# Seven block products instead of eight for the sparse values and six gate tiles, in a hybrid attention block on one core

## The chip, the core and the metric

The kernel runs on one core of a Trainium2 chip. Its engines are TensorE (PE in the profile, its weight loads PEld), VectorE (DVE), ScalarE (ACT), GpSimd (POOL) and SyncE (SP), which issues most DMAs. The metric is the device time of one execution in microseconds (us), lower is better.

## The reference, cut to what matters

One layer on x of 512 tokens by 1024 channels, float32. A normalised input h feeds one combined projection; dense attention (branch a) and sparse top-128 attention (branch b), 8 heads each, give outputs that are gated, projected and summed.

```
h = rmsnorm(x, norm_g)
(q_lat, c_kv, k_rope, z_a, q_b, k_b, v_b, z_b, q_idx, k_idx, w_idx, gate_a, gate_b) = split(h @ w_in)
y_a = mla_attention(...) * silu(z_a)
# sparse heads: score by an indexer, keep 128 keys, add a position bias
logits = q_b . k_sel * scale + bias ;  p = softmax(logits) ;  y_b = (p @ v_sel) * silu(z_b)
merged = sigmoid(gate_a) * (y_a @ w_o_a) + sigmoid(gate_b) * (y_b @ w_o_b)
out = rmsnorm(x + merged @ w_out)
```

## The kernel before

Everything lies transposed in SBUF (channels on partitions, 512 tokens along the free dimension). Each float32 operand is split in two rounded parts, hi (a ScalarE copy, line 291) and lo (a subtraction on VectorE, line 317, or on GpSimd, line 319). A product takes three matmuls per 128-row block of the contraction, hi.hi, hi.lo and lo.hi (`mm3`, line 394; the matmul itself is line 389). The normalised input is eight such pairs, `hT[0..7]`, tiles `s_h`.

The order of all instructions is made by a planner when the program is built (`Flow.run`, line 178): generator functions yield steps, each with one or more engines that could do it and a cost; the step that could start first is emitted. On the chip every engine then works through its list in that fixed order and waits on semaphores. A step with several engines goes to the one with the earliest planned end; `BOTH` is VectorE or GpSimd.

TensorE's filler is a queue of weight tiles (`QUEUE`, line 1641). `fetcher` (line 833) loads each into one of 4 raw buffers of 512 KB (`raw`), `splitter` (line 843) makes the hi and lo parts (`s_w`), `multiplier` (line 853) runs the products. One tile of a projection (`proj`, line 861) is 128 output channels: 24 matmuls of 512 columns with weights `s_w` and moving data `s_h`. The queue holds eight gate tiles of branch a (`ga`) and eight of branch b (`gb`), each stored as tanh in `s_sig`; eight silu tiles (`za`, `zb`); key and query tiles of the sparse heads (`sb`); and the sparse values (`vb`, `values`, line 918) in two halves of 96 matmuls of 256 columns, here with `s_h` as weights and `s_w` moving. Between the filler run, at higher priority, the heads: logits, softmax, four transposes by a matmul with the identity (line 406), the product with the values. Before the sparse heads VectorE does the top-128 search (lines 786 and 787, 16 rounds for each of three row tiles).

A sparse head (`dsa_head`, line 1236) adds a bias tile to the logits and takes their maximum in one VectorE operation (line 1248), negates the maximum (line 336), exponentiates on ScalarE with the row sum, takes the reciprocal (line 1142) and scales the row by it (`normalise`, on VectorE line 347 or GpSimd line 350). Its bias tile plus mask is prepared by `dsa_base` (line 1223). Its query and key operands come from `dsa_jobs` (line 1195): for each head of a pair separately the 64 rows are split by ScalarE and VectorE (qhi and s_op), the keys then copied to the other 64 partitions by DMA.

After the last projection (`hT_done`, line 881, key "projections") come the branch output products `branch_out` (line 1335), for a and then b, eight tiles of 12 matmuls each, and the output product, already done with seven block products (`output`, line 1491). `y_gate` (line 1275) splits the gated head outputs for them.

Of the kernel before, what the change touches and what calls it, by code (L numbers as in the profile page):

```python
# [79 lines left out]
class Step:  # L80


    moves = 0.0
    pair = False
    pbias = None
# [45 lines left out]
class Flow:  # L131
# [46 lines left out]
    def run(self, stop=None):  # L178
        while self.threads:
            if stop and stop():  # L180
                return
            moved = False
            for t in sorted(self.threads, key=lambda t: t.prio):
                if isinstance(t.req, Get):
                    b = t.req.pool.give(t.req)
                    if b is not None:
                        self.advance(t, b)
                        moved = True
                elif isinstance(t.req, Until) and t.req.cond():
                    self.advance(t, None)  # L190
                    moved = True
            if moved:
                continue
            best = None
            for t in self.threads:
                if isinstance(t.req, Step):
                    for i, (eng, dur, emit) in enumerate(t.req.options):
                        s = self.start(t.req, eng)
                        key = (s + BIAS * t.prio, t.prio)
                        if len(t.req.options) > 1:  # L200
                            fin = s + dur + {"POOL": self.pbias if t.req.pbias is None else t.req.pbias, "ACT": ABIAS}.get(eng, 0.0)
# [12 lines left out]
            if eng == "SP":  # L214

                self.free["SP"] = s + 0.05
                self.hw = max(self.hw, s) + (0.65 if step.ins and step.outs else 0.475)
                self.dma = max(self.dma, self.hw + 0.65) + dur
                end = self.dma + (2.2 if step.ins and step.outs else 1.0)
# [12 lines left out]
            self.advance(t, None)  # L232
# [1 line left out]

RAW_LAG = {"DVE": 0.125, "POOL": 0.1, "ACT": 0.1}
BIAS = 0.01
ABIAS = 0.0
TC_ARGS = {}


# [1 line left out]
def tile_block(ctx: ExitStack, tc: tile.TileContext, a: dict, out: bass.AP, bias_dram: bass.AP):  # L242
# [11 lines left out]
    rounded = {"w", "wo", "xg", "h", "qs", "th", "lat", "op", "qpe", "ph", "last", "vv", "ys", "mg", "oh"}  # L254
    uid = [0]

    def fresh(b, cls):
# [202 lines left out]
    rb = fixed("rb", [64, NH])  # L460
    rbs = fixed("rbs", [64, NH], F32R)
    TOK = [slice(t * P, (t + 1) * P) for t in range(NT)]
    SWAP = [(k + 16) % 32 for k in range(32)]
    done = set()

# [357 lines left out]


    jobs = []

    class Job:
        def __init__(self, src, widths, body, cls="w", cap=None, prep=None):
# [14 lines left out]
    def splitter():  # L843
        for job in jobs:
            yield Until(lambda: job.raw is not None)
            if job.prep:
                spawn(job.prep(job), 9)
# [13 lines left out]
    def proj(name, c, take, prio):  # L861
# [14 lines left out]
        left[0] += 1  # L876
        Job(a[name][c], [512, 512], body)

    left = [0]

    def hT_done():
# [5 lines left out]

    sig = {}

    def gate(name, c):  # L890


        def take(ps):
            s = yield slot("sig")
            yield act(s.all.f, ps.all, AF.Tanh, scale=0.5)
            put(ps)
            sig[name, c] = s

        proj(name, c, take, 12)

    zt = {}

    def silu2(name, c):


        def take(ps):
# [3 lines left out]
            put(ps)  # L910
            zt[name, c] = z

        proj(name, c, take, 11)


    vv, vv_users = {}, {}
# [221 lines left out]
        put(ps, t)  # L1138
        done.add((br, h))

    def normalise(p, mx):
        yield Step([("DVE", 0.07, lambda: nc.vector.reciprocal(mx.tile[:, 3:4], mx.tile[:, 2:3]))], [mx], [mx])  # L1142
        yield scale_by(p, p, mx[:, 3:4], NORM)

    def prob_tiles(cls, cap):
        s = []
# [45 lines left out]
    lanes = {"a": set(), "b": set()}  # L1192


    def dsa_jobs(j):
        def take_q(ps):
            yield Until(lambda: ("a", NH - 1, 0) in operands)
            for b in range(2):
                own, oth = slice(64 * b, 64 * b + 64), slice(64 - 64 * b, 128 - 64 * b)
                q = yield Get(QHI)  # L1200
                yield act(q[own, :], ps[own, :], AF.Copy, scale=HD ** -0.5)
                yield stt(q[oth, :], ps[own, :], HD ** -0.5, q[own, :].f, ALU.mult, ALU.subtract)
                operands["b", 2 * j + b, 0] = q
            put(ps)

        def take_k(ps):
            for b in range(2):
                own, oth = slice(64 * b, 64 * b + 64), slice(64 - 64 * b, 128 - 64 * b)
                kh = yield slot("op")
                kl = yield slot("op")  # L1210
                yield act(kh[own, :], ps[own, :])
                yield lo_part(kl[own, :], ps[own, :], kh[own, :])
                yield dma(kh[oth, :].f, kh[own, :].f)
                yield dma(kl[oth, :].f, kl[own, :].f)
                operands["b", 2 * j + b, 1] = (kh, kl)
            put(ps)

        proj("w_kb", j, take_k, 8)
        proj("w_qb", j, take_q, 8)

    bases = {}

    def dsa_base(h):
# [4 lines left out]
        yield dma(bias.all.f, bass.AP(bias_dram.tensor, h * NREL + 1, [[1, P], [1, S]]))  # L1228
        slots, probs = yield from prob_tiles("p", 6)
        for i in range(NT):  # L1230
            n = P * (i + 1)
# [4 lines left out]
    def dsa_head(h):  # L1236
# [7 lines left out]
        def soft(i, ps):  # L1244
            n = P * (i + 1)
            mx = yield Get(SMALL)
            p = probs[i]
            step = Step([("DVE", 0.1 + 0.00104 * n, lambda: nc.vector.tensor_tensor_reduce(
                p.ap, ps.tile[:, :n], p.ap, op0=ALU.add, op1=ALU.max, scale=1.0, scalar=FILL,
                accum_out=mx.tile[:, 0:1]))], [mx, p.buf], [ps])  # L1250
# [24 lines left out]
    def y_gate(br, j):  # L1275
# [21 lines left out]


    left1, left2, left3, left4, base = {}, {}, {}, {}, {}
    LO, HI = slice(0, 256), slice(256, 512)  # L1300

    def split_m(x, n, dst, key):
        hi = yield slot("mg")
# [267 lines left out]

    outs = [(p, c) for p, n in ((1, 2), (7, 4), (2, 2), (6, 2), (5, 4), (4, 2), (3, 2)) for c in range(n)]
    for item in QUEUE.split():
        kind, n = item[:2], item[2:]
        if kind == "ga" or kind == "gb":
            gate("w_" + kind, int(n))
        elif kind == "za" or kind == "zb":
            silu2("w_" + kind, int(n))
        elif kind == "pe":
            qpe_job()  # L1580
        elif kind == "ma":
            mla_job(int(n))
        elif kind in ("va", "vb"):
            values(kind[1], int(n))
        elif kind == "sb":
            dsa_jobs(int(n))
        elif kind == "ou":
            out_job(*outs.pop(0))
    for m in range(2 * NK):
# [27 lines left out]
    for br in "ab":  # L1617
        for j in range(4):
            spawn(y_gate(br, j), 8)
    spawn(final_loads(), 20)  # L1620
    spawn(output(), 15)
    run()


LATE = 0.5
PSQ = 0.0
PSET = 0.0
NORM = ('DVE', 'POOL')
NWARM = 7
XAT = 1  # L1630
QPOOL = 0
PHCAP = 4
WCAP = 8
TCAP = 5
# [89 lines left out]
```

## Time and profile before

| | us |
|---|---|
| median of 3 runs | 439.57 (439.42 to 441.98) |
| the profiled execution | 439.49 |
| its span, first to last instruction | 437.7 |
| PE, DVE, ACT, POOL busy | 426.2, 345.1, 244.6, 125.3 |

The granted TensorE clock is 0.998 of full speed. Times in the profile count from the span's start. In a group's row "x768 | 189.4, 394" means 768 instructions, 189.4 us in which at least one of them ran, and 394 ns for one from its start to its end; matmuls overlap, so what one costs in a stream is the distance between starts.

### The profile page before, as it was taken

How to read it: one execution, taken by the hardware profiler on the slowest of the kernel's cores; microseconds unless marked ns; L12 is line 12 of the kernel's file. 1: busy time of each engine (PE TensorE's matmuls, PEld its weight loads, DVE VectorE, ACT ScalarE, POOL GpSimd, SP SyncE). 2: the span in 40 equal slices, each digit the busy share in tenths (PEclk: the TensorE clock that was granted, in tenths of full speed). 3: DMA queues.
4: the chain of work that ended last, by engine and by line, in shares of the span. 5: the costliest groups of instructions: out<-in, count | busy, mean ns of one | idle time of the engine just before them, and what ended most of it. 6: DMA issues, size and time to landing. Idle time of an engine off the chain costs nothing.

```text
span 437.7 us, 6862 instructions
## 1 busy us (share of the span) xinstructions
PE 426.2 (97%) x2219; PEld 364.7 (83%) x2219; DVE 345.1 (79%) x810; ACT 244.6 (56%) x546; POOL 125.3 (29%) x150
## 2 busy tenths in 40 slices
PE   8999999999999999999999999999999999999994
PEld 5899878888887888878899888998888888888883
DVE  5599589999999999794343977835776686999995
ACT  6976877557472757364333654734565553345633
POOL 2256966544555634000003120050000011001452
PEclk9999999999999999999999999999999999999999
DMA  8973441725337361414541216234116445538405
GB/s 260 393 251 92 111 146 55 204 82 138 98 84 209 79 185 33 120 43 144 145 148 45 73 73 144 82 112 133 60 50 216 168 152 185 179 111 288 145 1 192
DMA packets 26500, 59.45 MB, mean 136 GB/s; under 512 B 4072, under 2 KB 4600, under 8 KB 26464
## 3 DMA queue, kind: packets, MB, share of 16 engines
q1 hardware_dynamic: 25744, 58.05, 43.2%
q0 software_dynamic: 576, 0.83, 0.7%
q8 instruction: 17, 0.28, 0.3%
q14 instruction: 19, 0.16, 0.1%
q10 hardware_dynamic: 144, 0.13, 0.1%
HBM read 48.39 MB, written 2.12 MB: 115 GB/s over the span
## 4 chain that ended last, share of the span: by engine, by line
PE 73%; DVE 13%; DMA 4%; ACT 4%; issue 2%; POOL 1%; SPq 1%; POOLq 0%; DVEq 0%; ACTq 0%
PE ps L389 67%; PE ps L406 4%; DVE mask L787 3%; DVE sm L786 3%; DMA s_op<-s_op 2%; DVE sm L1163 1%; DMA raw<-w_kvl 1%; DMA s_op<-kpel 1%; ACT junk L300 1%; PE ps L764 1%; SPq L416 1%; DVE s_ph L317 1%; PE ps L1182 1%; DVE qhi L328 1%; DVE s_op L328 1%
## 5 line engine op out<-in xcount | busy, mean ns | idle before, releaser
L389 PE MATMUL ps<-s_h,s_w 128*128 128x512 f32 x768 | 189.4, 394 | 0.0
L389 PEld LDWEIGHTS ps<-s_h,s_w 128*128 128x128 f32 x768 | 140.9, 188 | 26.7 <-issue 0.2
L319 POOL TENSOR_TENSOR s_w<-raw,s_w 128x512 fp32r<-128x512 f32 (+2 forms) x38 | 45.1, 1197 | 99.0 <-DMA raw<-w_out 64.3
L291 ACT CAST s_w<-raw 128x512 fp32r<-128x512 f32 (+3 forms) x114 | 64.3, 591 | 4.2 <-PE ps L389 2.1
L317 DVE TENSOR_TENSOR s_w<-raw,s_w 128x512 fp32r<-128x512 f32 (+2 forms) x76 | 49.2, 670 | 12.2 <-ACT s_w L291 11.8
L319 POOL TENSOR_TENSOR s_p<-s_bias,mask 128x128 f32<-128x128 f32 (+3 forms) x19 | 14.4, 785 | 102.9 <-DMA s_bias<-bias_scratch 90.3
L389 PE MATMUL ps<-s_ys,s_w 128*128 128x512 f32 x192 | 43.7, 389 | 0.0
L389 PEld LDWEIGHTS ps<-s_ys,s_w 128*128 128x128 f32 x192 | 36.0, 188 | 7.5
L389 PE MATMUL ps<-s_wo,s_mg 128*128 128x512 f32 (+1 forms) x156 | 33.0, 373 | 0.0
L389 PE MATMUL ps<-s_w,s_xg 128*128 128x328 f32 (+1 forms) x192 | 32.4, 324 | 0.0
L389 PEld LDWEIGHTS ps<-s_w,s_xg 128*128 128x128 f32 x192 | 31.5, 188 | 0.8 <-DVE s_w L317 0.2
L389 PEld LDWEIGHTS ps<-s_wo,s_mg 128*128 128x128 f32 x156 | 27.6, 188 | 5.2
L787 DVE MATCH_REPLACE8 mask<-sm,mask 128x256 f32<-128x256 f32 (+2 forms) x48 | 25.9, 541 | 0.0
L786 DVE MAX8 sm<-mask 128x8 f32<-128x256 f32 (+2 forms) x48 | 25.6, 549 | 0.3
L300 ACT ACTIVATE s_p<-ps,sm 128x128 f32<-128x128 f32 (+3 forms) x32 | 16.8, 527 | 15.2 <-DVE sm L1163 13.4
L389 PE MATMUL ps<-s_w,s_h 128*128 128x256 f32 x192 | 23.8, 284 | 0.0
L389 PEld LDWEIGHTS ps<-s_w,s_h 128*128 128x128 f32 x192 | 23.4, 192 | 0.2
L300 ACT ACTIVATE s_p<-s_p,sm 128x128 f32<-128x128 f32 (+3 forms) x32 | 17.8, 558 | 9.9 <-DVE sm L336 9.8
L406 PE MATMUL ps<-ident,s_p 128*128 128x128 f32 x160 | 22.9, 273 | 0.0
L300 ACT ACTIVATE s_sig<-ps 128x512 f32<-128x512 f32 x16 | 9.6, 597 | 22.7 <-PE ps L389 22.5
L350 POOL TENSOR_SCALAR s_p<-s_p,sm 128x128 f32<-128x128 f32 (+3 forms) x31 | 16.1, 527 | 19.0 <-DVE sm L1142 18.8
L389 PE MATMUL ps<-s_lat,s_w 128*128 128x512 f32 x78 | 21.4, 398 | 0.0
(164 smaller groups left out, 723.5 us busy)
## 6 DMA issues: line engine op xcount, KB each, us to landing
raw<-w_out SPq DMA_DIRECT2D x18, 512.0 KB, 4.2
raw<-w_ga SPq DMA_DIRECT2D x8, 512.0 KB, 4.3
raw<-w_gb SPq DMA_DIRECT2D x8, 512.0 KB, 3.6
raw<-w_o SPq DMA_DIRECT2D x16, 256.0 KB, 3.8
s_op<-s_op SPq DMA_DIRECT2D x28, 128.0 KB, 2.3
s_x<-xT SPq DMA_DIRECT2D x8, 256.0 KB, 5.4
s_xn<-x SPq DMA_DIRECT2D x8, 256.0 KB, 5.4
raw<-w_za SPq DMA_DIRECT2D x4, 512.0 KB, 4.2
```

The lines of the kernel that those rows point to most:

```text
L291: nc.scalar.copy(dst.ap, src.ap)
L300: nc.scalar.activation(dst.ap, src.ap, func, **kw)
L317: opts.append(("DVE", 0.07 + 0.00104 * x.n, lambda: nc.vector.tensor_tensor(dst.ap, x.ap, y.ap, op=op)))
L319: opts.append(("POOL", 0.15 + 0.0021 * x.n, lambda: nc.gpsimd.tensor_tensor(dst.ap, x.ap, y.ap, op=op)))
L328: lambda: nc.vector.scalar_tensor_tensor(dst.ap, x.ap, sc(s), y.ap, op0=op0, op1=op1))],
L350: lambda: nc.gpsimd.tensor_scalar(dst.ap, x.ap, s.ap, 1.0, ALU.mult, ALU.mult)))
L389: nc.tensor.matmul(ps.ap, l.ap, r.ap, start=start and i == 0, stop=stop and i == len(pairs) - 1, skip_group_check=more)
L406: nc.tensor.transpose(d.ap, s.ap, ident.tile)
L416: return Step([("SP", n / 360000.0, lambda: nc.sync.dma_start(d, s))], bufs(dst), bufs(src))
L764: yield pe(0.005 + n / 2400, [ps.all], [qs[h].all, ks[0].all], lambda: nc.tensor.matmul(ps.tile[:, :n], qs[h].tile[:96, TOK[i]], ks[0].til ...
L786: yield Step([("DVE", t, lambda: nc.vector.max(m8.tile, work.tile))], [m8], [work])
L787: yield Step([("DVE", t, lambda: nc.vector.match_replace(work.tile, m8.tile, work.tile, MARK))], [work], [m8])
```

## The change

- **Values.** The two halves `vb0`, `vb1` become one job `VB` (`values2`): the 512 x 1024 by 1024 x 512 product is cut in 2 by 2 blocks and done with seven block products (numbers 1 to 7) instead of eight, each 24 matmuls of 256 columns.
- **Six gate tiles.** `gb0` to `gb5` become three pairs (`proj2`); the two weight tiles of a pair are the blocks of one side, seven products of 12 matmuls of 256 columns instead of 48 of 512. `gb6`, `gb7` stay as they were.
- **What seven products need.** `input_sums` makes eight sums and differences of halves of `hT` (tiles `s_tmp`) and their hi and lo parts (`s_hs`); `prep` sums the raw weights in place and in `s_wsum`, and splits seven blocks where there were four; `seven` combines the products (`s_pair`), some in PSUM by accumulating into a bank that another engine has just read, some by VectorE additions.
- **Sparse heads.** Line 1248 gives negated logits and their minimum, so the negation of the maximum goes; the scaling by the reciprocal may go to VectorE or ScalarE, no more to GpSimd (`NORM_B`). Queries and keys of a pair are split by one operation of 128 partitions each instead of two of 64, and more DMAs move the halves in place.
- **Gates of branch a.** All eight (`AWAY`) are written to DRAM after their tanh and read back after the last projection (`fetch_gates`).
- One of three copies of each index query goes by GpSimd's queue (`QPOOL`), the planner counts 1.5 us more for the bias load, `y_gate` waits for the last pair instead of the last projection, and the queue has another order.

How the counts of instructions change, from the two built programs (TensorE: operands moving, weights; the rest of TensorE's list is the same in number):

```
PE   ps<-s_h,s_w   128x512: 768 -> 624      DVE  s_wsum, raw sums 512: 8 -> 27 (one more on POOL)
PE   ps<-s_h,s_w   128x256:   0 -> 108      DVE  s_tmp sums 512: 0 -> 6, 256: 0 -> 13 ; s_hs 512: 0 -> 7
PE   ps<-s_hs,s_w  128x256:   0 -> 144      DVE  s_pair<-ps 256: 0 -> 15, 512: 0 -> 5
PE   ps<-s_w,s_h   128x256: 192 ->  72      DVE  s_w<-raw or s_wsum 512: 62 -> 73
PE   ps<-s_w,s_hs  128x256:   0 ->  96      DVE  s_p<-s_bias,mask: 13 -> 29 (POOL 19 -> 3)
ACT  s_p<-s_p,sm (scaling): 0 -> 18         DVE  s_p<-s_p,sm (scaling): 33 -> 14
ACT  s_w, s_hs casts 512: 90 -> 113         DVE  sm<-sm (negation): 32 -> 0
SP   s_op<-s_op: 28 -> 36, qhi: 0 -> 12     DVE  qhi, s_op splits of 64 partitions: 16 -> 0, of 128: 0 -> 8
SP   bias_scratch<-s_sig: 0 -> 8, back: 0 -> 8 ; s_qs<-s_th: 24 -> 16 (POOL 0 -> 8)
```

```diff
+    def input_sums():
+        yield Until(lambda: sums_due[0] in done)
+        for k in range(4):
+            f = []
+            for i in (k, k + 4):
+                t = yield slot("tmp", TCAP)
+                yield soon(tt(t.all.f, hT[i][0].all.f, hT[i][1].all.f, ALU.add, BOTH))
+                f.append(t)
+            x, y = (t.all.f for t in f)
+            yield soon(tt(x[:, HI], x[:, LO], x[:, HI], ALU.subtract, BOTH))
...
+    def proj2(first, second):
...
+        def prep(job):
...
+            yield from split_t(1, b11)
+            t = yield slot("wsum")
+            t3 = t.all.f
+            yield soon(tt(t3, b22, b12, ALU.subtract, BOTH))
+            yield soon(tt(b12, b12, b11, ALU.subtract, BOTH))
+            yield soon(tt(b11, t3, b11, ALU.add, BOTH))
+            yield from split_t(6, b11)
+            yield from split_t(2, b21)
+            yield from split_t(7, t3)
...
+    def seven(times, part, c11, c21, c12, c22, end):
...
+        x = yield bank("mm")
+        yield from times(1, x)
+        spawn(take("1", act(c22, part(x))), 0)
+        y = yield bank("mm")
+        yield from times(6, y)
+        yield Until(lambda: "1" in sums)
+        spawn(take("u2", add(c12, y, c22)), 0)
+        yield from times(2, x, True)
+        spawn(take("c11", act(c11, part(x)), x), 0)
+        yield Until(lambda: "u2" in sums)
+        yield from times(7, y, True)
+        spawn(take("u3", add(c21, y, c22), y), 0)
+        z = yield bank("mm")
+        yield from times(5, z)
+        yield Until(lambda: "u3" in sums)
+        spawn(take("c22", add(c22, z, c21)), 0)
+        v = yield bank("mm")
+        yield from times(4, v)
+        yield Until(lambda: "c22" in sums)
+        spawn(take("c21", add(c21, v, c21), v), 0)
+        yield from times(3, z, True)
+        spawn(take("c12", add(c12, z, c12), z), 0)
...
+    def fetch_gates():
+        yield is_done("projections")
+        for c in away:
+            yield is_done(("spilt", c))
             s = yield slot("sig")
+            yield dma(s.all.f, spilt(c))
+            sig["w_ga", c] = s
...
-            yield ts(mx[:, 1:2], mx[:, 0:1], -1.0, None, ALU.mult)
-            yield act(p, p, AF.Exp, bias=mx[:, 1:2], scale=1.0, accum=mx[:, 2:3])
-            yield from normalise(p, mx)
+            yield act(p, p, AF.Exp, bias=mx[:, 1:2], scale=-1.0, accum=mx[:, 2:3])
+            yield from normalise(p, mx, NORM_B)
...
-        yield is_done("projections")
+        yield is_done("pairs")
...
-QUEUE = 'ga0 ga1 pe ma0 va0 ga2 za0 ma1 va1 ga3 za1 ma2 ga4 za2 ma3 ga5 za3 sb0 zb0 ga6 ga7 sb1 zb1 vb0 gb1 gb0 sb2 zb2 vb1 gb2 sb3 gb3 zb3 gb4 gb5 ou gb6 ou gb7 ou'
+QUEUE = 'ga0 ga1 pe ma0 va0 ga2 za0 ma1 va1 ga3 za1 ma2 ga4 za2 ma3 ga5 za3 sb0 zb0 ga6 ga7 sb1 VB GB0 GB1 sb2 zb1 GB2 GB3 sb3 zb2 GB4 GB5 ou zb3 gb6 ou gb7 ou'
```

More of the change, by code (lines that the diff above doesn't have):

```diff
@@ L80 @@
 class Step:
+    abias = 0.0
+    late = 0.0
     moves = 0.0
@@ L218, in run @@
                 self.dma = max(self.dma, self.hw + 0.65) + dur
-                end = self.dma + (2.2 if step.ins and step.outs else 1.0)
+                end = self.dma + (2.2 if step.ins and step.outs else 1.0) + step.late
             else:
@@ L253, in tile_block @@
     slots = ctx.enter_context(tc.tile_pool(name="slots", bufs=1, reuse_waits="tile"))
[L254 removed]
+    rounded = {"w", "wo", "xg", "h", "qs", "th", "lat", "op", "qpe", "ph", "last", "vv", "ys", "mg", "oh", "hs"}
     uid = [0]
@@ L846, in splitter @@
             if job.prep:
-                spawn(job.prep(job), 9)
+                if job.body:
+                    yield from job.prep(job)
+                else:
+                    spawn(job.prep(job), 9)
                 continue
@@ L877, in proj @@
         Job(a[name][c], [512, 512], body)
+    hs = {}
+    def input_sums():
[8 more added lines that the diff above has]
+            yield soon(tt(x[:, HI], x[:, LO], x[:, HI], ALU.subtract, BOTH))
+            yield soon(tt(y[:, HI], y[:, HI], x[:, HI], ALU.subtract, BOTH))
+            yield soon(tt(x[:, LO], y[:, HI], x[:, LO], ALU.add, BOTH))
+            yield soon(tt(y[:, LO], y[:, LO], y[:, HI], ALU.subtract, BOTH))
+            for i in range(2):
+                hi = yield slot("hs")
+                lo = yield slot("hs")
+                yield act(hi.all, f[i].all.f)
+                yield soon(lo_part(lo.all, f[i].all.f, hi.all))
+                put(f[i])
+                hs[k, i] = (hi, lo)
@@ new lines, in side, with hold, split_t, times @@
+    def side(n, k):
+        if n in (1, 2, 4):
+            return cut(hT[k if n == 1 else k + 4], HI if n == 4 else LO)
+        return cut(hs[k, n in (3, 6)], HI if n in (6, 7) else LO)
+    def proj2(first, second):
+        parts, raws = {}, []
+        def hold(job):
+            raws.append(job.raw)
+            yield Until(lambda: True)
+        def split_t(n, x):
+            hi = yield slot("w", PCAP)
+            lo = yield slot("w", PCAP)
+            yield act(hi.all, x)
+            yield soon(lo_part(lo.all, x, hi.all))
+            parts[n] = (hi, lo)
+        def prep(job):
+            yield Until(lambda: raws)
+            raws.append(job.raw)
+            b11, b21 = raws[0][:, :S], raws[0][:, S:]
+            b12, b22 = raws[1][:, :S], raws[1][:, S:]
+            yield from split_t(1, b11)
[7 more added lines that the diff above has]
+            yield from split_t(7, t3)
+            put(t)
+            yield from split_t(5, b12)
+            yield soon(tt(b21, b21, b11, ALU.subtract, BOTH))
+            yield from split_t(4, b21)
+            put(raws[0])
+            yield from split_t(3, b22)
+            put(raws[1])
+        def times(n, ps, more=False):
+            for k in range(4):
+                yield Until(lambda: n in parts and (k, 0) in hs and (k, 1) in hs)
+                yield mm3(ps[:, :256], cut(parts[n], slice(k * P, k * P + P)), side(n, k), k == 0 and not more, k == 3, more)
+            put(*parts[n])
+        def body(job):
+            out = []
+            for _ in range(2):
+                out.append((yield slot("pair")))
+            views = [o.all.f[:, c] for o in out for c in (LO, HI)]
+            yield from seven(times, lambda ps: ps[:, :256], views[0], views[1], views[2], views[3], lambda: spawn(give(out), 3))
+            pair_done()
+        def give(out):
+            for o, (name, c, take, prio) in zip(out, (first, second)):
+                spawn(take(o), prio)
+            return
+            yield
+        left[0] += 1
+        pairs_left[0] += 1
+        Job(a[first[0]][first[1]], [512, 512], None, prep=hold)
+        Job(a[second[0]][second[1]], [512, 512], body, prep=prep)
@@ new lines, in seven, with take, add @@
+    def seven(times, part, c11, c21, c12, c22, end):
+        sums = set()
+        def take(key, step, release=None):
+            yield step
+            if release:
+                put(release)
+            sums.add(key)
+            if len(sums) == 7:
+                end()
+        def add(dst, ps, y):
+            return tt(dst, part(ps), y, ALU.add)
+        x = yield bank("mm")
[20 more added lines that the diff above has]
+        spawn(take("c12", add(c12, z, c12), z), 0)
@@ L879, in tile_block, with in_pairs @@
+    pairs_left = [0]
+    waiting = []
+    def in_pairs(item):
+        waiting.append(item)
+        if len(waiting) == 2:
+            proj2(*waiting)
+            waiting.clear()
     left = [0]
@@ L911, in take @@
             zt[name, c] = z
-        proj(name, c, take, 11)
+        how(name, c, take, 11)
     vv, vv_users = {}, {}
@@ L1192, in tile_block, with dsa_jobs @@
     lanes = {"a": set(), "b": set()}
-    def dsa_jobs(j):
+    def dsa_jobs(j, how=proj):
         def take_q(ps):
             yield Until(lambda: ("a", NH - 1, 0) in operands)
[L1198 to L1203, printed above, removed]
-            put(ps)
-        def take_k(ps):
[L1207 to L1215, printed above, removed]
-            put(ps)
-        proj("w_kb", j, take_k, 8)
-        proj("w_qb", j, take_q, 8)
+            q = yield Get(QHI)
+            q2 = yield Get(QHI)
+            lo = yield slot("op")
+            yield from split_scaled(q.all, lo.all, ps.all, HD ** -0.5)
+            put(ps)
+            first, second = slice(0, 64), slice(64, 128)
+            yield dma(q2[second, :].f, q[second, :].f)
+            yield dma(q2[first, :].f, lo[second, :].f)
+            yield dma(q[second, :].f, lo[first, :].f)
+            put(lo)
+            operands["b", 2 * j, 0] = q
+            operands["b", 2 * j + 1, 0] = q2
+        def take_k(ps):
+            first, second = slice(0, 64), slice(64, 128)
+            pairs = []
+            hi = yield slot("op")
+            lo = yield slot("op")
+            yield act(hi.all, ps.all)
+            yield lo_part(lo.all, ps.all, hi.all)
+            put(ps)
+            for part in (hi, lo):
+                k = yield slot("op")
+                for rows in (first, second):
+                    yield dma(k[rows, :].f, part[first, :].f)
+                yield dma(part[first, :].f, part[second, :].f)
+                pairs.append(k)
+            operands["b", 2 * j, 1] = tuple(pairs)
+            operands["b", 2 * j + 1, 1] = (hi, lo)
+        how("w_kb", j, take_k, 8)
+        how("w_qb", j, take_q, 8)
@@ L1227, in dsa_base @@
         bias = yield slot("bias")
-        yield dma(bias.all.f, bass.AP(bias_dram.tensor, h * NREL + 1, [[1, P], [1, S]]))
+        step = dma(bias.all.f, bass.AP(bias_dram.tensor, h * NREL + 1, [[1, P], [1, S]]))
+        step.late = 1.5
+        yield step
         slots, probs = yield from prob_tiles("p", 6)
@@ L1628 @@
 NORM = ('DVE', 'POOL')
+NORM_B = ('DVE', 'ACT')
+NORM_BIAS = -0.5
 NWARM = 7
 XAT = 1
-QPOOL = 0
+QPOOL = 1
 PHCAP = 4
```

141 lines of the change are left out of this document (123 added, 18 removed).

## The prediction

> **What bounds the kernel now.** I read the page first: span, busy time by engine, the chain that ended last.
>
> ```profile
> span 437.7 us, 6862 instructions
> PE 426.2 (97%) x2219; PEld 364.7 (83%) x2219; DVE 345.1 (79%) x810; ACT 244.6 (56%) x546; POOL 125.3 (29%) x150
> PE 73%; DVE 13%; DMA 4%; ACT 4%; issue 2%; POOL 1%; SPq 1%; POOLq 0%; DVEq 0%; ACTq 0%
> ```
>
> TensorE bounds it. The question is where it idles and where the other engines have room for new work, so next the windows: length, then PE, PEld, DVE, ACT, POOL busy with instruction counts.
>
> ```profile
> 0.00:20.00 20.00, 17.18 (x85) 13.62 (x86) 9.46 (x22) 15.12 (x35) 4.67 (x16) 1.00 0.92 320
> 54.00:76.00 22.00, 21.47 (x101) 16.86 (x100) 19.59 (x35) 17.16 (x38) 14.88 (x16) 1.00 0.35 104
> 76.00:174.00 98.00, 97.40 (x527) 83.12 (x526) 97.03 (x265) 57.55 (x142) 50.08 (x64) 1.00 0.45 122
> 174.00:196.00 22.00, 21.53 (x106) 17.97 (x105) 18.45 (x59) 12.23 (x30) 0.00 (x0) 1.00 0.33 93
> 196.00:236.00 40.00, 40.00 (x225) 35.12 (x224) 16.89 (x29) 14.46 (x27) 3.35 (x4) 1.00 0.41 125
> 236.00:279.00 43.00, 42.90 (x238) 37.28 (x237) 34.83 (x113) 26.07 (x64) 5.06 (x7) 1.00 0.30 82
> 279.00:310.00 31.00, 31.00 (x183) 27.52 (x182) 15.47 (x27) 12.35 (x23) 5.93 (x7) 1.00 0.45 134
> 310.00:326.00 16.00, 15.53 (x87) 13.27 (x86) 13.63 (x51) 10.26 (x29) 0.00 (x0) 1.00 0.10 33
> 326.00:347.00 21.00, 21.00 (x94) 17.35 (x93) 12.87 (x21) 11.15 (x21) 0.00 (x0) 1.00 0.50 167
> 347.00:425.00 78.00, 78.00 (x357) 65.06 (x356) 71.73 (x126) 37.67 (x73) 15.26 (x7) 1.00 0.47 158
> ```
>
> From 76 to 174 (dense heads, top-128 search) VectorE is as full as TensorE: 97.0 of 98. From 174 to 347, where the sparse heads, the values and the gates of b run, it works 112.1 (the six rows' sum) of 173, so 61 us are free. From 347 the branch and output products run, TensorE without a gap; this part is unchanged. The tail after TensorE does not change either:
>
> ```profile
> 329.86 94.96 PE ps L389 x430
> 424.84 1.38 DVE s_xr L328 x2
> ```
>
> The price of a matmul is the distance between starts, from TensorE's timeline (start, us, form):
>
> ```profile
> 196.18 26.13 PE L389 MATMUL ps<-s_h,s_w 128*128 128x512 f32 x114
> 222.14 11.68 PE L389 MATMUL ps<-s_w,s_h 128*128 128x256 f32 x96
> 233.66 2.92 PE L389 MATMUL ps<-s_h,s_w 128*128 128x512 f32 x12
> 277.62 10.32 PE L389 MATMUL ps<-s_w,s_h 128*128 128x256 f32 x84
> 287.77 2.92 PE L389 MATMUL ps<-s_h,s_w 128*128 128x512 f32 x12
> ```
>
> 512 columns: (222.14 - 196.18)/114 = 0.2277 us. 256 columns: (233.66 - 222.14)/96 = 0.1200 and (287.77 - 277.62)/84 = 0.1208, mean 0.1204. Two points give 0.0131 us fixed and the rest by columns, so halving a matmul costs little here.
>
> **The change part by part. TensorE.** Six tiles of 24 matmuls of 512 columns go: -144 x 0.2277 = -32.8 us. 256-column matmuls go from 192 to 420: three pairs of 84 come, and the values go from 192 to 168; 228 x 0.1204 = +27.45. Sum -5.3 us: -2.9 from the values, -2.45 from the pairs. It is direct where TensorE has no gap, as in the windows above.
>
> Weighed against that: the Trainium skill, "TensorE: Matmul & The Clock Gate", section "Back-to-back issue gap", says that in a stream weight load and matmul set the spacing together, and gives 81 ns at 128 columns and 131 ns at 512. A straight line would put 256 columns at 98 ns (an estimate from that page), and the sum would be -144 x 131 + 228 x 98 ns = +3.5 us: a loss. The rows above disagree with it for these operands at both widths.
>
> **VectorE.** Starts in a busy stretch give its prices:
>
> ```profile
> 380.33 0.69 DVE L317 TENSOR_TENSOR s_wo<-s_wsum,s_wo 128x512 fp32r<-128x512 f32 x1
> 380.93 0.69 DVE L317 TENSOR_TENSOR s_mg<-s_sig,s_mg 128x512 fp32r<-128x512 f32 x1
> 384.72 0.41 DVE L317 TENSOR_TENSOR s_sig<-s_sig 128x256 f32<-128x256 f32 x1
> 385.05 0.68 DVE L328 SCALAR_TENSOR_TENSOR s_sig<-s_sig,ps 128x512 f32<-128x512 f32 x1
> ```
>
> 0.60 us for 512 columns, 0.33 for 256. New: 19 weight sums, 13 of h (6 sums, 7 lo parts), 11 more splits, 5 combinations of 512: 48 x 0.60 = 28.8; 13 sums and 15 combinations of 256: 28 x 0.33 = 9.2; 16 bias additions that were GpSimd's, a mean of 0.33: 5.3. Gone: 8 splits (16 of 64 partitions become 8 of 128) x 0.60 = 4.8; 32 negations and 19 scalings:
>
> ```profile
> L336 DVE TENSOR_SCALAR sm<-sm 128x1 f32<-128x1 f32 x32 | 4.1, 143 | 0.1
> L347 DVE TENSOR_SCALAR s_p<-s_p,sm 128x512 f32<-128x512 f32 x9 | 4.6, 513 | 0.1
> ```
>
> 4.1 us, and at most 19 x 0.51, since most are narrower; I take 0.3 each, 5.7. Net 43.3 - 14.6 = about +29 us. By the new order some two fifths of the growth (sums of h, run as the dense heads end) lie ahead of the sparse heads, in the full stage: the first sparse heads start some 11 us later, and there the order puts 99 matmuls of 512 columns (22.5 us) ahead of them where it had 48 (10.9 us). That hides it; uncovered it would cost the 11. The rest, about 18, goes into 61 free us.
>
> **Where a wait is new.** In each of four block jobs TensorE accumulates into a bank that another engine must first have read: product 2 after ScalarE's copy, 7 and 3 after VectorE's additions. One product lies between: 24 x 0.1204 = 2.9 us for values, 12 x 0.1204 = 1.45 for a pair. The reader sits in a fixed queue between 0.60-us splits, and a PE wait stops all behind it, heads too. No such wait exists before; the nearest row is TensorE waiting for one VectorE operation:
>
> ```profile
> PE ps L389 <- DVE qhi L328: 0.9, 2, 0.5
> ```
>
> 12 waits at 0 to 0.47 each (0.9/2): 0 to 5.6 us. Between is free time enough (a pair's 11 split-and-sum operations, 6.6 us, fit in its 10.1), so I take two late ones, +0.9. Below zero it cannot go.
>
> **Sparse heads.** Those two 0.47 are themselves the old query split, four steps in a row, for instance
>
> ```profile
> 185.13 0.60 ACT qhi L300
> 185.75 0.69 DVE qhi L328
> 186.47 0.60 ACT qhi L300
> 187.10 0.70 DVE qhi L328
> ```
>
> One ScalarE and one VectorE step take their place, so -0.9; but the second head then needs two DMAs in turn, the keys likewise.
>
> ```profile
> s_op<-s_op SPq DMA_DIRECT2D x28, 128.0 KB, 2.3
> s_bias<-bias_scratch SPq DMA_DIRECT2D x8, 256.0 KB, 4.1
> raw<-w_gb SPq DMA_DIRECT2D x8, 512.0 KB, 3.6
> raw<-w_o SPq DMA_DIRECT2D x16, 256.0 KB, 3.8
> ```
>
> 2 x 2.3 = 4.6 us instead of none for queries and 2.3 for keys; filler stands ahead in the order, so 0 (uncovered, 4.6 once per pair). SP issues 20 more of these; what queues behind are the raw weights of the values, which in the first two pairs wait behind copies that wait on VectorE. Negation, minimum for maximum, and ScalarE's scaling shift no PE work: 0.
>
> **Spilled gates.** 16 DMAs of 256 KB. The eight reads follow the last projection on SP; the first gate is due when the first branch product ends (12 x 0.2277 = 2.7 us) and blocks TensorE only when three banks are full, 8.2 us; it lands after 4.1. Six branch weights were issued ahead, 16.4 us of work, so those queued behind the reads have time. 0; if it were late, up to 4. **QPOOL**: eight index copies go to GpSimd, 14.9 of 22 us busy there; 0, with 1 us either way.
>
> **Sum.** 437.7 - 5.3 + 0.9 - 0.9 = 432.4 us span. The profiled execution took 439.49 us, 1.8 outside its span, and stands 0.1 below the median of 439.57. So 432.4 + 1.8 = 434.2 us.
>
> **The rivals.**
> - *VectorE is late at the hand-overs.* All 12 waits cost 0.47: 434.2 - 0.9 + 5.6 = 438.9, almost all of the gain. For it: the order puts about 0.85 us of VectorE work beside each us of products in these jobs, where windows now show 15.5 of 31 and 16.9 of 40. Against: each product of slack is twice or more a 0.60-us operation.
> - *Raw staging starves TensorE* (the other side). The values take all four raw buffers until they are summed, so the next pair cannot be fetched ahead. If each of four jobs starts one landing late, 4 x 3.6 = 14.4 us: 434.2 + 14.4 = 448.6. It decides from 1.3 us per job on (gain gone) and makes it slower by over 1% from about 2.4. Against: buffers come free one by one while seven products run.
> - *The heads gain more.* With VectorE's work smoothed and fewer steps per head, the idle time that TensorE now shows from 76 to 326 (0.6 + 0.5 + 0.1 + 0.5 = 1.7) goes, and no hand-over is late: 437.7 - 5.3 - 1.7 + 1.8 = 432.5; as much again in short gaps that busy time hides gives 430.8.
> - *Half-wide matmuls pay more among other work.* The fixed part would have to be 5.3/84 = 63 ns larger than 13: no gain, 439.5. The two 256-column rows speak against; the skill's spacing above is this case.
>
> **How the numbers follow.** Forecast 0.52 (own range 432.5 to 436), late hand-overs 0.19, starving 0.10, heads 0.17, half-wide 0.02. A measurement of this kernel tells about 1% from no change, 4.4 us: faster is below 435.2. Three quarters of the forecast (0.40) and the heads (0.17) are below: 0.57. The rest of the forecast, late hand-overs and half-wide make 0.33 within 1%; starving 0.10 slower. The range runs from 430.8 (heads) to 439.5, no gain at all, and leaves out little but starving.
>
> **What would show it.** 256-column products at 0.12 us in TensorE's timeline and its work 5.3 us less; TensorE's waits on `s_pair` (VectorE and ScalarE) under 1 us in sum, 5 or more for the first rival; waits of ScalarE or VectorE on `raw<-w_gb` and a gap of TensorE ahead of product 1 for starving; VectorE near 374 us busy; TensorE without a gap where the gates come back. I am wrong if TensorE's work falls by much less than 5, or if stalls of the sparse stage grow beyond 2 us.

## The result and the profile after

The changed kernel takes 435.33 us (median of 4 runs, 434.61 to 436.08), the kernel before 439.62 beside it: ratio 0.9892, 95% interval 0.9874 to 0.9909. The two medians alone give 0.9902, 4.3 us or 1.0% less; one of the four runs of before took 441.98. The result stands 1.1 us above the 434.2 predicted, and 0.1 above 435.2, the line below which the prediction called it faster. The profiled execution took 435.09 us for a span of 433.3, so 1.8 lie outside it, as before.

The page of the changed kernel: span, busy time by engine, the chain that ended last.

```profile
span 433.3 us, 7175 instructions
PE 420.7 (97%) x2303; PEld 364.6 (84%) x2303; DVE 382.5 (88%) x842; ACT 263.1 (61%) x590; POOL 131.7 (30%) x152
PE 51%; DVE 26%; issue 8%; ACT 5%; POOL 4%; DMA 4%; SPq 1%; POOLq 0%; DVEq 0%; ACTq 0%
```

PE is busy 5.5 us less, the span is 4.4 shorter, and DVE has grown by 37.4 us. DVE's share of the chain has doubled from 13 to 26%; whether that makes it a bound, one of the experiments asks. The windows (length, then PE, PEld, DVE, ACT, POOL):

```profile
54.00:76.00 22.00, 20.93 (x99) 16.18 (x97) 20.65 (x33) 15.56 (x34) 16.38 (x20) 1.00 0.48 142
76.00:174.00 98.00, 95.95 (x522) 82.25 (x521) 96.97 (x266) 59.08 (x147) 54.30 (x67) 1.00 0.48 128
174.00:196.00 22.00, 21.94 (x99) 17.68 (x99) 21.78 (x35) 11.73 (x22) 10.53 (x9) 1.00 0.55 150
196.00:236.00 40.00, 40.00 (x256) 36.37 (x256) 34.81 (x79) 23.66 (x52) 0.00 (x0) 1.00 0.45 135
236.00:279.00 43.00, 42.50 (x275) 38.58 (x274) 39.61 (x90) 28.50 (x64) 2.30 (x2) 1.00 0.41 114
279.00:310.00 31.00, 31.00 (x190) 27.96 (x190) 26.43 (x68) 18.63 (x45) 3.90 (x3) 1.00 0.48 140
310.00:326.00 16.00, 15.97 (x123) 15.28 (x123) 13.43 (x43) 12.83 (x34) 1.30 (x1) 1.00 0.28 101
```

Two things stand in it. From 174 to 326, where the block products run, TensorE idles 0.6 of 152 us (the five rows: 0.06, 0, 0.50, 0, 0.03); the same rows of before idle 1.0. From 54 to 174, which the block products do not touch, it idles 3.1 us (1.07 and 2.05), where before had 1.1 (0.53 and 0.60). So something was lost ahead of the part that the change is about. TensorE's waits in the changed kernel (releaser, sum, times, longest):

```profile
PE ps L485 <- DVE junk L444: 1.5, 1, 1.5
PE ps L766 <- DVE mask L329: 1.4, 1, 1.4
PE ps L766 <- DVE s_qs L318: 1.0, 1, 1.0
PE ps L407 <- POOL rstd L368: 0.8, 1, 0.8
PE ps L390 <- DVE s_pair L318: 0.5, 1, 0.5
```

The waits on `mask` and `s_qs`, 2.4 us in sum, belong to the scores of the indexer (line 766), at 77 and 55 us. The hand-overs, waits on `s_pair`, cost 0.5 in sum. The waits on the query split (`qhi`, 0.9 before) are gone.

The same by stage, for the whole span. TensorE's work is its number of matmuls in a stage times their price (0.0135 us plus 0.417 ns a column, which gives the rows' 0.120 and 0.227), and what is left of the stage is lost time, short gaps included:

| | before | after |
|---|---|---|
| to the end of the dense heads: length = work + lost | 175.9 = 160.7 + 15.2 | 177.8 = 160.0 + 17.8 |
| to the first branch product | 173.1 = 166.8 + 6.3 | 167.0 = 162.2 + 4.9 |
| the rest | 88.7 = 82.0 + 6.7 | 88.5 = 82.0 + 6.5 |

Work fell by 5.3, losses in the sparse stage by 1.4, and the first stage lost 2.6 more.

### The profile page after: what moved, and what is told of

It reads as the page before. It is cut to its first block, busy times and chain, and to the rows that moved or that the text cites. A ratio compares the mean times of both kernels' runs of the same rounds, so it can differ in the third digit from the quotient of the medians.

```text
span 433.3 us, 7175 instructions
## 1 busy us (share of the span) xinstructions
PE 420.7 (97%) x2303; PEld 364.6 (84%) x2303; DVE 382.5 (88%) x842; ACT 263.1 (61%) x590; POOL 131.7 (30%) x152
## 4 chain that ended last, share of the span: by engine, by line
PE 51%; DVE 26%; issue 8%; ACT 5%; POOL 4%; DMA 4%; SPq 1%; POOLq 0%; DVEq 0%; ACTq 0%
PE ps L390 47%; DVE mask L789 3%; DVE sm L788 3%; PE ps L407 3%; DVE sm L1430 2%; DVE s_mg L318 2%; DVE s_wo L318 2%; ACT s_w L292 2%; DVE s_ph L318 1%; DMA raw<-w_kvl 1%; SPq L417 1%; DVE s_pair L318 1%; DVE s_wsum L318 1%; DMA s_op<-s_op 1%; ACT junk L301 1%
## 5 line engine op out<-in xcount | busy, mean ns | idle before, releaser
L390 PE MATMUL ps<-s_h,s_w 128*128 128x512 f32 (+1 forms) x732 | 169.1, 378 | 0.0
L390 PEld LDWEIGHTS ps<-s_h,s_w 128*128 128x128 f32 x732 | 128.5, 188 | 22.4 <-issue 0.3
L292 ACT CAST s_w<-raw 128x512 fp32r<-128x512 f32 (+3 forms) x124 | 71.2, 591 | 21.7 <-DVE raw L318 9.6
L320 POOL TENSOR_TENSOR s_w<-raw,s_w 128x512 fp32r<-128x512 f32 (+2 forms) x41 | 50.7, 1244 | 88.2 <-ACT s_w L292 70.5
L318 DVE TENSOR_TENSOR s_w<-raw,s_w 128x512 fp32r<-128x512 f32 (+2 forms) x83 | 55.1, 679 | 10.6 <-ACT s_w L292 9.2
L301 ACT ACTIVATE s_p<-s_p,sm 128x384 f32<-128x384 f32 (+3 forms) x50 | 26.1, 546 | 5.3 <-DVE sm L1528 5.0
L390 PE MATMUL ps<-s_hs,s_w 128*128 128x256 f32 x144 | 20.6, 286 | 0.5 <-DVE s_pair L318 0.5
L407 PEld LDWEIGHTS ps<-ident,s_p 128*128 128x128 f32 x160 | 18.9, 140 | 2.1
L320 POOL TENSOR_TENSOR s_p<-s_bias,mask 128x128 f32<-128x128 f32 (+2 forms) x3 | 2.6, 867 | 57.7 <-DMA s_bias<-bias_scratch 57.7
L390 PEld LDWEIGHTS ps<-s_hs,s_w 128*128 128x128 f32 x144 | 18.7, 190 | 1.0 <-DVE s_pair L318 0.7
```

The costliest lines, as they stand in the source:

```text
L292: nc.scalar.copy(dst.ap, src.ap)
L301: nc.scalar.activation(dst.ap, src.ap, func, **kw)
L318: opts.append(("DVE", 0.07 + 0.00104 * x.n, lambda: nc.vector.tensor_tensor(dst.ap, x.ap, y.ap, op=op)))
L320: opts.append(("POOL", 0.15 + 0.0021 * x.n, lambda: nc.gpsimd.tensor_tensor(dst.ap, x.ap, y.ap, op=op)))
L390: nc.tensor.matmul(ps.ap, l.ap, r.ap, start=start and i == 0, stop=stop and i == len(pairs) - 1, skip_group_check=more)
L407: nc.tensor.transpose(d.ap, s.ap, ident.tile)
```

## The experiments

Times are medians; each ratio is to the kernel before on the same chip, with its 95% interval. They stand in the order of the argument.

**One block product of a kind at a time.** The theory: values and pairs each save their TensorE work, and the changed heads are neutral. In the queue a lower-case name is the plain projection.

`heads_only`, neither block product, the rest of the change kept:

```diff
-QUEUE = '... sb1 VB GB0 GB1 sb2 zb1 GB2 GB3 sb3 zb2 GB4 GB5 ou ...'
+QUEUE = '... sb1 vb0 vb1 gb0 gb1 sb2 zb1 gb2 gb3 sb3 zb2 gb4 gb5 ou ...'
-    spawn(input_sums(), PSUMS)
-        yield is_done("pairs")
+        yield is_done("projections")
```

> The changed kernel with the values in two halves by eight products and gb0 to gb5 as single tiles: sparse heads, spilled gates and index copies stay changed, no sums are made. Theory A (the gain is TensorE's work in the block products, 5.3 us, and the rest is neutral or a small loss ahead of the sparse heads): 439 to 441 us, no gain on the kernel before's 439.6. Rival B (the relief of VectorE in the sparse heads brings the gain, the block products little): 435 to 437.

438.72 us, 0.9986 (0.9972 to 0.9999): 0.9 less than before, just below theory A's range and well above B's.

`values_only`, `VB` kept, the gates as in `heads_only`:

> The changed kernel with only the values by seven products. A: 24 matmuls of 256 columns less than with neither, 2.9 us below the run with the heads alone. Rival B (VectorE's new work, some 17 us of it for the sums of h alone, is paid for): no faster than the heads alone.

437.78 us, 0.9955 (0.9943 to 0.9967): only 0.9 less than `heads_only` (1.4 by the ratios), not 2.9.

`pairs_only`, the pairs kept, the values as in `heads_only`:

> The changed kernel with only the six gate tiles in pairs. A: 2.45 us below the run with the heads alone. B: no faster than it, since three pairs have nine hand-overs and the sums of h for 2.45 us of TensorE.

441.34 us, 1.0038 (1.0024 to 1.0053): slower than before. The parts measured alone do not add up to the whole, so something other than TensorE's work differs between these kernels.

**The copies on GpSimd's queue.** `qpool0` is the changed kernel with one number undone: the index copies go by SyncE again.

```diff
-QPOOL = 1
+QPOOL = 0
```

> The changed kernel with all index copies on SP's queue again. Theory A2 (the front lost about 2.5 us because GpSimd's copies and its hold on VectorE delay the index scores): 433 to 434.5 us, and TensorE's waits for the mask and s_qs (1.4 and 1.0 us) go. Rival (SP's queue then delays the dense heads' operands, or the loss comes from VectorE's own load): 435 to 437.

433.36 us, 0.9854 (0.9842 to 0.9867): 2.0 us faster than the whole change, and the best of all kernels here that compute the reference; its interval lies below that of the changed kernel. Its page, and all waits of its TensorE:

```profile
span 431.6 us, 7180 instructions
PE 421.7 (98%) x2303; PEld 366.4 (85%) x2303; DVE 378.0 (88%) x845; ACT 262.0 (61%) x588; POOL 124.1 (29%) x143
```

```profile
PE ps L485 <- DVE junk L444: 1.5, 1, 1.5
PE ps L407 <- ACT s_p L301: 0.6, 2, 0.3
PE ps L390 <- ACT s_xg L301: 0.5, 1, 0.5
PE ps L407 <- POOL s_latraw L351: 0.5, 2, 0.2
PE ps L407 <- POOL s_p L351: 0.4, 1, 0.4
```

Both waits of line 766 are gone. So is the one on `s_pair`.

`before_qpool1` puts the same number into the kernel before (`QPOOL = 0` to `1`):

> The kernel before with one of three copies of each index query on GpSimd's queue, nothing else. Theory A2 (that copy is itself the loss in the front): 441 to 442.5 us, and the two waits of TensorE at the index scores (about 1.4 and 1.0 us) appear. Rival (it only hurts with the changed kernel's other work): 439 to 440.

440.86 us against 439.47, 1.0031 (1.0019 to 1.0042): 1.4 us slower, 0.1 below the range of theory A2. Its TensorE timeline (start, us, form, the wait and its releaser) has both waits, where the kernel before has neither:

```profile
55.36 0.56 PE L764 MATMUL ps<-s_qs,s_qs 96*128 96x256 f32 x2 [0.99 <-DVE s_qs L317]
77.79 0.50 PE L764 MATMUL ps<-s_qs,s_qs 96*128 96x512 f32 x1 [1.39 <-DVE mask L328]
```

So that number costs 1.4 us without the block products and 2.0 with them. What makes the smaller wait was not followed up. Where the larger one comes from, the changed kernel's VectorE and GpSimd show side by side:

```profile
73.46 0.47 DVE L329 SCALAR_TENSOR_TENSOR mask<-ps,widx,mask 128x256 f32<-128x256 f32 x1
73.85 3.27 DVE L318 TENSOR_TENSOR s_tmp<-s_tmp,s_tmp 128x512 f32<-128x512 f32 x1
77.04 1.26 DVE L329 SCALAR_TENSOR_TENSOR mask<-ps,widx,mask 128x384 f32<-128x384 f32 x2
```

```profile
73.46 0.54 POOL L421 DMA_DIRECT2D s_qs<-s_th  x1
74.02 1.31 POOL L320 TENSOR_TENSOR s_tmp<-s_tmp,ropes 128x512 f32<-128x512 f32 x1
75.27 1.29 POOL L320 TENSOR_TENSOR s_w<-raw,s_w 128x512 fp32r<-128x512 f32 x1
```

An addition of two SBUF tiles takes 3.27, where operations of its form take 0.69 by their median, and ends at 77.12, 0.56 after the second of GpSimd's two operations. Behind it in VectorE's fixed list stand the score operations that must read TensorE's bank, so the next score matmul waits 1.37. The Trainium skill, "SBUF — State Buffer", section "Who interferes with whom", has a mechanism for this: a VectorE operation with both inputs in SBUF shares a read port with a GpSimd operation that reads SBUF, and the one that is issued second stands until the first is done. By that section ScalarE never waits. The traces agree on who stands. Of all operations over 0.15 us longer than the median of their operation and shape, the excess is 13.6 us on VectorE here, 6.4 before, 5.3 in `qpool0`, and 0.0 on ScalarE in all three; each of the 20 on VectorE here overlaps one on GpSimd. (0.3 to 1.2 us of each sum may be no hold: those operations read PSUM and take the same time at each occurrence, 0.61 to 0.62 us at 384 columns.) The order of issue is not shown. The addition's record begins 0.17 us ahead of GpSimd's first operation, and the addition stands through both. In `qpool0` the planner put the score operations (`mask`, `s_op`) ahead of the additions:

```profile
74.53 1.85 DVE L329 SCALAR_TENSOR_TENSOR mask<-ps,widx,mask 128x256 f32<-128x256 f32 x3
76.34 0.69 DVE L329 SCALAR_TENSOR_TENSOR s_op<-ps,s_th 128x512 fp32r<-128x512 f32 x1
76.95 0.61 DVE L329 SCALAR_TENSOR_TENSOR mask<-ps,widx,mask 128x384 f32<-128x384 f32 x1
77.48 2.39 DVE L318 TENSOR_TENSOR s_tmp<-s_tmp,s_tmp 128x512 f32<-128x512 f32 x2
```

There too two additions take 2.39 instead of 1.3, but TensorE has no wait there. How much of the cost is the copies' time on GpSimd and how much the order that they lead to was not separated.

**The parts again, without that number.** `heads_only_q0`, `values_only_q0`, `pairs_only_q0` are the three kernels above with `QPOOL = 0`.

> The changed kernel with all index copies on SP and neither block product (values in halves, single gate tiles). With the index copies off GpSimd, theory A3 (the sparse heads' edits shorten the stalls of the sparse stage by about 1.5 us, the copies cost 1.4 to 2): 436.5 to 437.5 us. Theory A (heads neutral): 439 to 440.

438.15 us, 0.9962 (0.9948 to 0.9976).

> As the last, with the values by seven products. A: its 2.9 us in full, or less a little for the sums of h: about 434 to 435 if the heads alone stand near 437.

435.5 us, 0.99 (0.9879 to 0.9921).

> As the heads alone, with the six gate tiles in three pairs and the values in halves. A: 2.45 us less, about 434.5. Rival (pairs alone are eaten by their own waits, as with the copies on GpSimd, where they were 2.6 us slower than the heads alone): 437 or more.

439.64 us, 0.9993 (0.9978 to 1.0009). Theory A's 434.5 is missed, and the rival's 437 or more came.

Against their forms with the copies on GpSimd the three are 0.6, 2.3 and 1.7 us faster, so the cost of that number varies with the rest of the kernel. With `qpool0` these make a square: heads 438.15, with values 435.5, with pairs 439.64, with both 433.36. The values save 2.65, and 2.9 were predicted. The pairs cost 1.5 alone and save 2.1 beside the values. In the trace of `pairs_only_q0` TensorE has one long wait of the sparse stage, behind the last projections:

```profile
334.61 13.43 PE L390 MATMUL ps<-s_h,s_w 128*128 128x512 f32 x58 [2.25 <-DVE s_w L318]
```

It waits for weights split on VectorE, whose list there reads:

```profile
330.06 2.48 DVE L329 SCALAR_TENSOR_TENSOR s_ys<-s_y,s_ys 128x512 fp32r<-128x512 f32 x4
332.55 0.69 DVE L318 TENSOR_TENSOR s_y<-ps,s_tmp 64x512 f32<-64x512 f32 x1
333.26 0.69 DVE L329 SCALAR_TENSOR_TENSOR s_ys<-s_y,s_ys 128x512 fp32r<-128x512 f32 x1
333.87 2.49 DVE L318 TENSOR_TENSOR s_w<-raw,s_w 128x512 fp32r<-128x512 f32 x4
```

The head outputs' splits (`s_ys`, first needed by the branch products) stand in the list ahead of four weight splits that TensorE needs now; the wait ends at 334.61, when the first of the four is done. In `qpool0` the planner has it the other way round:

```profile
323.03 1.89 DVE L318 TENSOR_TENSOR s_w<-raw,s_w 128x512 fp32r<-128x512 f32 x3
327.89 2.48 DVE L329 SCALAR_TENSOR_TENSOR s_ys<-s_y,s_ys 128x512 fp32r<-128x512 f32 x4
```

Lost time in the sparse stage is 7.7 in `pairs_only_q0`, 4.6 in `heads_only_q0`: 3.1 more, of which this wait is 2.25, and after it the last stage loses another 1.2 (7.7 against 6.5). By these rows it is the planner's order that spoils the pairs alone, not their matmuls; no run fixes that order by hand. The same 2.24 wait stands in `pairs_only`.

`dve_bias` is `qpool0` with the additions of the bias tiles on VectorE alone, to see whether the few left on GpSimd hold VectorE up at the hand-overs:

```diff
-            yield tt(probs[i], backward(bias.all.f[:, :n]), mask[i].all, ALU.add, BOTH)
+            yield tt(probs[i], backward(bias.all.f[:, :n]), mask[i].all, ALU.add)
```

> The changed kernel with all index copies on SP (433.4 us) and all bias additions of the sparse heads on VectorE, so that GpSimd's reads stand less in VectorE's way in the sparse stage; a try at a faster version. Where the hold of one engine on the other matters there: 432.5 to 433; else 433.4 to 434.

435.49 us, 0.9898 (0.9874 to 0.9922): 2.1 slower than `qpool0`, a miss. Its trace shows a wait as long as that:

```profile
331.06 13.44 PE L390 MATMUL ps<-s_h,s_w 128*128 128x512 f32 x58 [2.24 <-DVE s_w L318]
```

The planner fell into the same order as in `pairs_only_q0`. Whether GpSimd's few additions matter at the hand-overs, this run can't tell.

**Is VectorE a bound now?** `no_sums_q0` is `qpool0` without the sums of the input and of the weights: the blocks are split and multiplied as they are, so TensorE's work is the same and the seven products no longer make up the product of the reference.

```diff
-    spawn(input_sums(), PSUMS)
-            yield soon(tt(t3, b22, b12, ALU.subtract, BOTH))
-            yield soon(tt(b12, b12, b11, ALU.subtract, BOTH))
-            yield soon(tt(b11, t3, b11, ALU.add, BOTH))
...
-            yield from split_t(7, t3)
+            yield from split_t(7, b22)
...
```

> The changed kernel with all index copies on SP (433.4 us), with the sums of h and of the weights left out: blocks are split and multiplied as they are, the combinations of products stay, and the result is not the reference's. It takes some 24 us of work from VectorE. Theory A (VectorE's sums lie in its free time): 432.5 to 433.5 us. Rival B (VectorE's load is paid for): 430 us or less.

432.9 us against 433.36 of `qpool0` (0.9849, 0.9835 to 0.9862; the intervals overlap). Its page:

```profile
PE 420.7 (98%) x2303; PEld 364.4 (84%) x2303; DVE 346.4 (80%) x787; ACT 257.2 (60%) x583; POOL 127.8 (30%) x146
```

31.6 us of VectorE's work are gone, and 0.5 us of time by the medians, which is inside the noise; theory B wanted 430 us or less. The sums are hidden, though VectorE has 25% of the chain in `qpool0`.

**The hand-overs bare.** `bare_q0` is `qpool0` with the products in the order 1, 2, 6, 7, 5, 3, 4 instead of 1, 6, 2, 7, 5, 4, 3: the same work, but no product between the read of a bank and the accumulation into it. The weight splits follow the new order, and some raw buffers come free one split later.

```diff
-        y = yield bank("mm")
-        yield from times(6, y)
         yield Until(lambda: "1" in sums)
-        spawn(take("u2", add(c12, y, c22)), 0)
         yield from times(2, x, True)
         spawn(take("c11", act(c11, part(x)), x), 0)
+        y = yield bank("mm")
+        yield from times(6, y)
+        spawn(take("u2", add(c12, y, c22)), 0)
         yield Until(lambda: "u2" in sums)
...
```

> The changed kernel with all index copies on SP (433.4 us), with the seven products in the order 1, 2, 6, 7, 5, 3, 4, so that no product lies between a bank's read and its next accumulation; same work. Theory A (a product of 1.45 or 2.9 us between hides the hand-overs): bare, each of 12 costs 0.6 to 1.0 us, 440 to 445 us, less where heads' matmuls fill in. Rival (hand-overs are cheap anyway): 434 to 436.

441.67 us, 1.0043 (1.003 to 1.0055): 8.3 us slower than `qpool0`. The waits of TensorE on the readers of its banks in sum, then the three of the values' job:

```profile
PE ps L390 <- DVE s_pair L318: 3.5, 3, 1.4
PE ps L390 <- ACT s_pair L292: 1.7, 3, 0.7
```

```profile
220.12 3.14 PE L390 MATMUL ps<-s_w,s_h 128*128 128x256 f32 x24 [0.68 <-ACT s_pair L292]
227.08 5.99 PE L390 MATMUL ps<-s_w,s_hs 128*128 128x256 f32 x48 [0.94 <-DVE s_pair L318]
234.49 3.11 PE L390 MATMUL ps<-s_w,s_hs 128*128 128x256 f32 x24 [1.43 <-DVE s_pair L318]
```

The sparse stage loses 13.9 instead of 5.4, 8.5 more. TensorE waits at six of the 12 hand-overs, 0.5 to 1.4 us each, 5.2 in sum. At the other six no wait is listed; in the pairs the heads' matmuls run in between. Part of the remaining 3.3 are longer waits of the heads on `s_p` (1.8 instead of 0.6); the rest was not followed up. With one product between, in `qpool0`, no wait on `s_pair` is listed at all. The one in the changed kernel, 0.50, ends at 251.58: VectorE's operation on the bank, at 251.10, comes behind a split that took 1.49 instead of 0.69 beside one of the GpSimd additions (249.52 to 250.52):

```profile
249.57 1.49 DVE L318 TENSOR_TENSOR s_w<-raw,s_w 128x512 fp32r<-128x512 f32 x1
251.10 0.42 DVE L318 TENSOR_TENSOR s_pair<-ps,s_pair 128x256 f32<-128x256 f32 x1
```

**The price of half-wide matmuls.** `half_wide` is the kernel before with the tiles `gb0` to `gb5` as 288 matmuls of 256 columns instead of 144 of 512, nothing else.

```diff
+                if name == "w_gb" and c < 6:
+                    for i in range(2):
+                        cols = slice(256 * i, 256 * i + 256)
+                        yield mm3(ps[:, cols], cut(job.parts[k // 4], slice(o, o + P)), cut(hT[k], cols), k == 0 and i == 0, k == NK - 1 and i == 1)
...
```

> The kernel before with gb0 to gb5 as 256-column matmuls, 288 instead of 144 of 512. Theory A (fixed cost 13 ns): +1.9 us, 441.5. Rival (half-wide matmuls pay 63 ns more among other work): +9 us or more.

441.65 us against 439.47, 1.0047 (1.0034 to 1.0061): 2.2 us for 144 more matmuls, 15 ns each (10 to 19 by the interval's ends), 13 predicted.

## Why the prediction held, and where it missed

- **TensorE's term, -5.3: right.** Work by count and price fell by 5.3. In the changed kernel's timeline of a pair's products, 12 matmuls of 256 columns take (240.04 - 238.60)/12 = 0.120 us each:

```profile
238.60 1.60 PE L390 MATMUL ps<-s_h,s_w 128*128 128x256 f32 x12
240.04 1.60 PE L390 MATMUL ps<-s_hs,s_w 128*128 128x256 f32 x12
241.48 1.60 PE L390 MATMUL ps<-s_h,s_w 128*128 128x256 f32 x12
```

  The rival of dearer half-wide matmuls needed 63 ns more than the 13 on each of the 84 that come on top (or 5.3/228 = 23 ns on each new half-wide one); `half_wide` shows 15 in all. That rival stood beside the Trainium skill, "TensorE: Matmul & The Clock Gate", section "Back-to-back issue gap": by the estimate from its figures the change would have been a loss of 3.5. The 0.120 us here, where that estimate had 98 ns, decides against it for these operands.
- **VectorE's added load hidden: right.** Busy 382.5, "near 374" predicted; about 7 of the growth of 37.4 is not added work but the longer operations (excess 13.6 against 6.4). The filler covers the start of the sparse heads as told: 99 matmuls without a gap, and the first sparse logits 13 us later (11 estimated), first row before, the others after:

```profile
186.98 0.40 PE L389 MATMUL ps<-s_op,qhi 128*128 128x256 f32 x2
```

```profile
177.90 22.64 PE L390 MATMUL ps<-s_h,s_w 128*128 128x512 f32 x99
200.38 0.64 PE L390 MATMUL ps<-s_op,qhi 128*128 128x256 f32 x4
```

- **Hand-overs, +0.9: about right, at too low a price.** 0.5 in the changed kernel, none listed in `qpool0`. A late one was priced at 0 to 0.47; the bare ones that TensorE waits for cost 0.5 to 1.4, and it was the product between that made the term small, as argued. "No such wait exists before" is right of waits and not of hand-overs. The output product of the kernel before accumulates into banks that are read first (lines 1517 and 1564), always with a product between, and there TensorE is busy 78.00 of 78 us.
- **Sparse heads, -0.9: right in sign.** `heads_only_q0` stands 1.5 below before, and the query split's waits are gone. The gates, the new order of the queue and the other small edits are in that 1.5 too, and were not taken apart.
- **Starving, no late gates: right.** TensorE waits for no raw weights and for no gate in the changed kernel. But a sibling of the starving rival does exist: weights split too late, 2.2 us, in the three kernels whose order puts the head outputs' splits first. The prediction did not have it.
- **QPOOL, "0, with 1 us either way": the step that failed.** It looked only at GpSimd's free time (14.9 of 22 us busy). It left out VectorE, whose operations take longer beside GpSimd's, and the order that the planner makes with the copies there: +1.4 in the kernel before, +2.0 in the changed one. Which of the two weighs more stays open. The condition "stalls of the sparse stage beyond 2 us" never came; the loss was in a stage that the sum had left untouched.

The terms, predicted and measured (differences of medians, each good to 0.6 to 0.9 us by the intervals):

| | predicted | measured |
|---|---|---|
| sparse heads and the rest without block products | -0.9 | -1.5 (439.62 to 438.15) |
| values and pairs, hand-overs included | -4.45 | -4.8 (438.15 to 433.36) |
| QPOOL | 0 | +2.0 (433.36 to 435.33) |
| sum | -5.35 | -4.3 |

The time came out nearer than the parts. The prediction missed by 1.1 us because the other two terms brought 0.95 us more than it said, and so made up for half of what QPOOL cost.

What stays open: whether values and pairs would save their full 5.35 under an order fixed by hand, since every kernel here was planned anew, and by what the planner comes to one order of `s_ys` and `s_w` or the other.

## What to carry to other kernels

Here the smaller number of products paid about its count on a TensorE that was the bound, with one whole product ahead of each accumulation into a bank that another engine must read first. Without that product the kernel lost 8.3 us and all of the gain. When matmuls are counted, look for such hand-overs and for what stands between. Where a planner orders the work, test each small switch by itself: one copy in three moved to another queue cost 2.0 us, almost half of the 4.8 that values and pairs brought. A part measured alone can lose where it gains beside the others, so look at the order before blaming the part.

## What was not expected of the hardware

- A VectorE addition of two SBUF tiles took 3.27 us instead of 0.69 while GpSimd ran two operations back to back, and 1.49 beside one.
- VectorE's share of the chain that ended last doubled from 13 to 26% (25% in `qpool0`), and yet taking 31.6 us of its work away from `qpool0` saved 0.5 us.
- With no product between (`bare_q0`), TensorE waits 0.5 to 1.4 us at six hand-overs of a bank to ScalarE or VectorE, more than the 0.37 to 0.42 us for which such an operation itself runs in the changed kernel (min/median/max in ns):

```profile
L318 DVE TENSOR_TENSOR s_pair<-ps,s_pair x20: 405/418/692, 224.4 to 327.1; 128x256 f32<-128x256 f32 x15, 128x512 f32<-128x512 f32 x5
L292 ACT COPY s_pair<-ps x8: 348/373/587, 221.5 to 317.2; 128x256 f32<-128x256 f32 x6, 128x512 f32<-128x512 f32 x2
```
